# Moving a small mask transfer from the shared load queue to the ScalarE queue, with longer PE filler behind it

## Chip, cores and metric

One core of one Trainium2 chip. The metric is the device time of one execution in microseconds, median of several. Kernel before: 91.02 us (90.93 to 91.16). Runs agree within a few tenths of a per cent, so 2% is far outside the noise. In the traces PE is TensorE, DVE VectorE, ACT ScalarE, POOL GpSimd and SP SyncE; SPq and ACTq are the queues on which SP and ACT issue transfers. A filler is a matmul on zeros whose result nobody reads.

## The reference

```python
def setup_inputs():
    batch, m, k, n = 16, 512, 512, 512
    ...
        "mask": (np.triu(np.ones((m, n))) == 0).astype(np.float32),   # x, weight: float32

def reference(x, weight, scale, mask):
    y = scale * np.matmul(x, weight)
    y = np.where(mask == 1, y, -1e9)
    y_exp = np.exp(y - np.max(y, axis=-1, keepdims=True))
    return (y_exp / np.sum(y_exp, axis=-1, keepdims=True)).astype(np.float32)
```

16 MiB of x go in and 16 MiB of output go out, in 16 "units" of 1 MiB each (half the rows of two neighbouring matrices of the batch), beside 1 MiB of weights and the mask. Only the four 128 x 128 diagonal blocks of the mask are loaded: 512 runs of 512 bytes.

## The kernel before

```python
def load(u):
    xf = x_pool.tile([P, T, K], FP32, name="xf")                 # X_BUFS = 8 of these
    seq(nc.sync.dma_start(xf.rearrange("p t k -> p (t k)"), x_r[u // 2, u % 2]))
...
def store(u):
    ot = ots[u % OUT_BUFS]
    seq(nc.sync.dma_start(out_r[u // 2, u % 2], ot.rearrange("p t n -> p (t n)")))

load(0)
seq(nc.sync.dma_start(w_f32, weight.rearrange("(p kt) n -> p kt n", kt=KT)))
load(1)
seq(nc.sync.dma_start(diag_f32, diag_r))                         # the mask
for u in range(2, X_BUFS):
    load(u)
...
spin(12)                                                         # filler matmuls on zeros: keep the PE clock up
make_identity(nc, ident_bf)
...                                                              # "spread": four copies of the identity on ACT
cast(0); transpose(0); spin(16); evict(0)
...                                                              # weights to bf16
cast(1); transpose(1); spin(8); evict(1)
seq(nc.vector.tensor_scalar(out=diag_bf, in0=diag_f32, ...))     # needs the mask
for t in range(T):                                               # "band": additive mask, used by every unit
    seq(nc.tensor.matmul(pm, lhsT=spread[:, t], rhs=diag_bf..., start=True, stop=True))
    ...
for u in range(U + 1):                                           # the main loop
    ...                                                          # transpose u+1, cast u+2, evict u+1
    multiply(u)                                                  # matmuls, band added by one more matmul, exp
    normalise(u - 1); store(u - 1)
    if u - 1 + X_BUFS < U:
        load(u - 1 + X_BUFS)
```

All loads and stores go through one queue, SP's, in this order ("the line" below). A load can be issued only when its buffer is free, so beyond the first eight each load is issued right behind a store.

The softmax here doesn't subtract the row's maximum and nothing guards it: scores larger than these inputs give would overflow.

## Time and profile before

| | before |
|---|---|
| time, us | 91.02 |
| span in the profile, us | 89.1 |
| PE busy | 83% |
| DMA in the 40 slices | 9 tenths nearly throughout |
| main loop starts, us | 16.19 |
| first store issued, us | 21.50 |
| last store issued / landed, us | 80.1 / 88.05 |

Read it as two engines running side by side: PE has work without a gap from 16.2 to 77.5 us, and the line of transfers has work from 2.2 to 87.7 us. The lines that show this are in the prediction.

### The profile page before, as it was taken

To read this page: it belongs to the slowest core of one execution; us is meant where nothing else is said; L and a number is where in the kernel's file an instruction comes from. 1 tells how busy PE (TensorE), PEld (TensorE's weight loads), DVE (VectorE), ACT (ScalarE), POOL (GpSimd) and SP (SyncE) were. 2 spreads that over 40 slices of the span, in tenths; PEclk is the share of its full clock that TensorE was granted. 3 is DMA by queue.
4 is the path that set the end of the run, shared out by engine and by line. 5 is a ranking of instruction groups with operands and counts; after the bars stand their busy time and mean duration, and the time that the engine had idled before them with its cause. 6 is when DMAs were issued, how large, how long until landed. Compare 5 with 4: busy or idle time off the path is not lost.

```text
span 89.1 us, 1666 instructions
## 1 busy us (share of the span) xinstructions
PE 74.3 (83%) x616; PEld 50.0 (56%) x616; DVE 60.3 (68%) x123; ACT 55.0 (62%) x154; POOL 7.3 (8%) x20
## 2 busy tenths in 40 slices
PE   4967979899999999999999999999999999700000
PEld 1315454685795598579659847964984784300000
DVE  5876263989499779949977977967494999080000
ACT  5402604977697686969768786977778796710000
POOL 7620000002001000200100020002000102000000
PEclk9999999999999999999999999999999999995555
DMA  1899779999999999999999999999999999999970
GB/s 22 313 408 431 293 289 438 419 431 419 427 419 431 419 431 419 416 419 431 423 427 412 434 427 423 423 431 423 419 416 445 416 427 419 434 419 427 434 316 33
DMA packets 5287, 34.97 MB, mean 393 GB/s; under 512 B 544, under 2 KB 1056, under 8 KB 1056
## 3 DMA queue, kind: packets, MB, share of 16 engines
q1 hardware_dynamic: 5280, 34.87, 94.2%
q8 instruction: 5, 0.08, 0.3%
q14 instruction: 2, 0.02, 0.0%
HBM read 18.09 MB, written 16.78 MB: 392 GB/s over the span
## 4 chain that ended last, share of the span: by engine, by line
PE 72%; DMA 10%; DVE 4%; SPq 1%; ACT 1%; DVEq 0%; issue 0%; ACTq 0%
PE py L117 47%; PE pt L93 15%; DMA xf<-in_x_dram 10%; PE py L126 8%; PE py L175 2%; DVE ot L153 1%; DVE xb L84 1%; SPq L79 1%; ACT ot L136 1%; SPq L163 1%; DVE band L226 0%; DVEq L272 0%; ACT band L226 0%; PE py L219 0%; DVE rinv L151 0%
## 5 line engine op out<-in xcount | busy, mean ns | idle before, releaser
L117 PE MATMUL py<-w_bf,xt 128*128 128x256 bf16 (+1 forms) x256 | 49.4, 326 | 0.3 <-ACT band L226 0.3
L136 ACT ACTIVATE ot<-py 128x256 f32<-128x256 f32 (+1 forms) x64 | 31.2, 493 | 7.3 <-PE py L126 7.1
L117 PEld LDWEIGHTS <-xt 128*128 128x128 bf16 x256 | 24.4, 98 | 12.6 <-issue 0.5
L104 ACT COPY xt<-pt 128x1024 bf16<-128x1024 bf16 x16 | 16.2, 1012 | 13.6 <-PE pt L93 9.4
L84 DVE CAST xb<-xf 128x2048 bf16<-128x2048 f32 x16 | 19.5, 1220 | 7.2 <-DMA xf<-in_x_dram 7.2
L153 DVE TENSOR_SCALAR ot<-ot,rinv 128x256 f32<-128x256 f32 (+1 forms) x64 | 23.5, 431 | 0.8
L93 PE MATMUL pt<-ident_bf,xb 128*128 128x128 bf16 x256 | 17.0, 219 | 1.7 <-DVE xb L84 1.7
L93 PEld LDWEIGHTS <-xb 128*128 128x128 bf16 x256 | 15.9, 114 | 3.6 <-DVE xb L84 2.7
L126 PE MATMUL py<-band,ident_bf 128*128 128x256 bf16 x64 | 17.4, 273 | 0.0
L103 DVE COPY xt<-pt 128x1024 bf16<-128x1024 bf16 x16 | 11.0, 686 | 6.4 <-PE pt L93 6.4
L136 ACT ACTIVATION_READ_ACCUMULATOR ot<-py 128x1 f32 x64 | 12.8, 200 | 0.0
L175 PE MATMUL py<-zeros 128*128 128x512 bf16 x36 | 10.3, 447 | 1.2 <-DVE zeros L170 1.2
L155 POOL MEMSET ot<- 2x256 f32 x8 | 3.6, 449 | 65.8 <-DVE ot L153 65.8
L126 PEld LDWEIGHTS <-ident_bf 128*128 128x128 bf16 x64 | 6.3, 98 | 4.1
L175 PEld LDWEIGHTS <-zeros 128*128 128x128 bf16 x36 | 3.9, 112 | 6.3 <-issue 2.7
L151 DVE RECIPROCAL rinv<-rsum 128x4 f32<-128x4 f32 x16 | 2.7, 168 | 2.6 <-ACT ot L136 2.6
L183 DVE MEMSET ot<- 128x1024 f32 x4 | 3.6, 912 | 0.6 <-issue 0.6
L226 DVE CAST band<-py 64x256 bf16<-64x256 f32 x4 | 1.4, 408 | 1.4 <-PE py L219 1.4
L226 ACT CAST band<-py 64x256 bf16<-64x256 f32 x4 | 1.4, 367 | 1.4 <-DVE band L226 1.4
L190 ACT ACT_TABLE_LOAD x1 | 1.3, 1283 | 0.7 <-PEq L258 0.7
L184 POOL MEMSET ot<- 2x256 f32 x4 | 1.2, 301 | 1.5 <-DVE ot L183 1.4
L190 ACT COPY spread<-ident_bf 128x128 bf16<-128x128 bf16 x4 | 1.0, 330 | 0.2 <-POOL ident_bf masks.py:199 0.2
(14 smaller groups left out, 6.7 us busy)
## 6 DMA issues: line engine op xcount, KB each, us to landing
xf<-in_x_dram SPq DMA_DIRECT2D x16, 1024.0 KB, 14.9
out_dram<-ot SPq DMA_DIRECT2D x16, 1024.0 KB, 12.1
w_f<-in_weight_dram SPq DMA_DIRECT2D x1, 1024.0 KB, 7.0
diag_f<-in_mask_dram SPq DMA_DIRECT2D x1, 256.0 KB, 10.5
```

The source lines that it names most:

```text
L84: seq(nc.vector.tensor_copy(xb, st_x.pop(u)))
L93: nc.tensor.transpose(st_pt[u][kt // 2][:, kt % 2, t], xb[:, t].rearrange("p (k kt) -> p kt k", kt=KT)[:, kt], ident_bf,)
L103: seq(nc.vector.tensor_copy(xt[:, 0:2], pt[0]))
L104: seq(nc.scalar.copy(xt[:, 2:4], pt[1]))
L117: nc.tensor.matmul(py[:, :NC], lhsT=xt[:, kt, t], rhs=w_bf[:, kt, :NC], start=(kt == 0), stop=(kt == KT - 1),)
L126: nc.tensor.matmul(py[:, h * HB : NC], lhsT=ident_bf, rhs=band[:, h, t], start=False, stop=True, skip_group_check=True,)
L136: nc.scalar.activation(out=ot[:, t, :NC], in_=py[:, :NC], func=AF.Exp, bias=0.0, scale=float(scale), accum_out=rsum[:, t : t + 1],)
L153: seq(nc.vector.tensor_scalar_mul(ot[:, t, :NC], ot[:, t, :NC], rinv[:, t : t + 1]))
L155: seq(nc.gpsimd.memset(ot[0:2, 0, :HB], 1.0 / N))
L175: seq(nc.tensor.matmul(idle, lhsT=zeros[:, :P], rhs=zeros, start=True, stop=True))
L183: nc.vector.memset(ots[i][:, :, HB:], 0.0)
L226: seq(copy(band[half, :, t, g * P : (g + 1) * P], src[half, :, g]))
```

## The change

The intent: take the slow little mask transfer out of the line of loads, give it ScalarE's (ACT's) queue, let it flow "beside" the big loads, and bridge PE's longer wait for it with filler.

```diff
     load(0)
     seq(nc.sync.dma_start(w_f32, weight.rearrange("(p kt) n -> p kt n", kt=KT)))
-    load(1)
-    seq(nc.sync.dma_start(diag_f32, diag_r))
-    for u in range(2, X_BUFS):
+    for u in range(1, X_BUFS):
         load(u)
 ...                      # after the four spread copies
+    seq(nc.scalar.dma_start(diag_f32, diag_r))
 ...                      # after transpose(1)
-    spin(8)
+    spin(20)
```

## The prediction

> **What bounds the kernel now.** I read the slices first, then the DMA stretches, then the timeline of the start, then the waits of the DMA-issuing engine, and only then the chain of waits, because here the chain misleads. From the page:
>
> ```profile
> PE   4967979899999999999999999999999999700000
> DVE  5876263989499779949977977967494999080000
> DMA  1899779999999999999999999999999999999970
> GB/s 22 313 408 431 293 289 438 419 431 419 427 419 431 419 431 419 416 419 431 423 427 412 434 427 423 423 431 423 419 416 445 416 427 419 434 419 427 434 316 33
> PE py L117 47%; PE pt L93 15%; DMA xf<-in_x_dram 10%; PE py L126 8%; PE py L175 2%; DVE ot L153 1%; DVE xb L84 1%; SPq L79 1%; ACT ot L136 1%; SPq L163 1%; DVE band L226 0%; DVEq L272 0%; ACT band L226 0%; PE py L219 0%; DVE rinv L151 0%
> ```
>
> PE is full from the seventh slice to the thirty-fourth and the chain gives it 72%. But the last compute instruction is over at 80.1 us and the span is 89.1: the last tenth belongs to DMA alone, and the DMA row is at 9 almost throughout, with one dip, in slices five and six. The stretches show that dip, the waits of the issuing queue show the tail:
>
> ```profile
> core 0: us, PE busy (x) PEld busy (x) DVE busy (x) ACT busy (x) POOL busy (x), PEclk, DMA share, GB/s
> 4.20:10.20 6.00, 4.73 (x32) 2.40 (x31) 3.59 (x5) 1.83 (x2) 0.60 (x2) 1.00 1.00 419
> 10.20:12.40 2.20, 1.73 (x11) 0.65 (x9) 1.23 (x1) 0.13 (x1) 0.00 (x0) 1.00 0.58 160
> 12.40:85.00 72.60, 64.79 (x572) 45.82 (x570) 52.63 (x114) 50.81 (x147) 3.59 (x8) 0.97 1.01 425
> ```
>
> ```profile
> SPq L272 <- DMA out_dram<-ot: 7.3, 1, 7.3
> ```
>
> So all transfers form one line, served at 425 GB/s, and the kernel ends 7.3 us after the last store was issued because that store stands behind others. In the trace's landing records the last two stores land at 85.61 and 88.05, 2.44 us apart, which is 1 MiB at full rate: still a backlog. The first bound is the DMA line; PE is a second bound close behind it. In the middle they touch: the casts of the last four x tiles, up to the one at 68.51 us, each start on a landing, yet PE never runs dry.
>
> The start, from the timeline:
>
> ```profile
> 2.18 0.96 ACT L190 COPY spread<-ident_bf 128x128 bf16<-128x128 bf16 x4 [0.16 <-POOL ident_bf masks.py:199]
> 2.69 0.70 SPq L165 DMA_DIRECT2D diag_f<-in_mask_dram  x1
> 10.97 1.23 DVE L84 CAST xb<-xf 128x2048 bf16<-128x2048 f32 x1 [1.75 <-DMA xf<-in_x_dram]
> 12.26 1.08 PE L93 MATMUL pt<-ident_bf,xb 128*128 128x128 bf16 x16 [0.47 <-DVE xb L84]
> 13.18 1.89 PE L175 MATMUL py<-zeros 128*128 128x512 bf16 x8
> 13.54 0.42 DVE L207 TENSOR_SCALAR diag_bf<-diag_f 128x512 bf16<-128x512 f32 x1
> 14.91 1.03 PE L219 MATMUL py<-diag_bf,spread 128*128 128x512 bf16 x4
> 16.19 0.60 PE L117 MATMUL py<-w_bf,xt 128*128 128x256 bf16 x4 [0.26 <-ACT band L226]
> ```
>
> The mask is issued at 2.69 and, by its row of the issues (10.5 us to landing), lands at 13.2, in time: the conversion at 13.54 does not wait for it. Converted at 13.96, it is ready before the eight filler matmuls end (the chain starts L219 at 15.07). The main loop starts at 16.19.
>
> **What the Trainium skill says.** (1) "DMA: Bandwidth & Descriptors", section "Issuing engines are not separate DMA queues": transfers from the scalar and sync engines run on the same 16 DMA engines and interleave; a second issuer only saves sequencer time. No run yet shows a second queue here; the issue costs 0.6 to 0.7 us. (2) Same page, "Queues, rings and completion order": each DMA engine takes turns between the queues that have work, a packet at a time. The trace of before has one data queue and cannot confirm it; my landing time for the mask rests on it. (3) Same page, "Why small descriptors are slow (HBM only)": small descriptors cost a fixed overhead each. The trace shows far more than that: the mask is 512 packets of 512 B, 32 per engine, mostly 27 ns each, so 0.86 us an engine, but x tile 1 and x tile 2, with the mask between, land 4.67 us apart where neighbours are 2.48 apart. The mask takes 2.19 us of the line; some 1.3 us of that the engines stand idle. (4) "TensorE: Matmul & The Clock Gate", "Wait — 56ns, not 53.3ns?": 215.7 ns from start to start for N = 512 with a warm clock. The trace agrees: eight fillers take 15.07 - 13.34 = 1.73 us on the chain, 0.216 each.
>
> **The change part by part.**
>
> The mask leaves the SP line. It is now the fifth instruction of ACT, right after the four spread copies, with no semaphore wait before it (the instruction order shows this). So it is issued at about 2.18 + 0.96 = 3.15, only 0.45 us later than before, but on a queue of its own: it no longer stands behind w and x tile 1, it alternates with them. ACT is idle until its eviction at 8.37, so 0.7 us of issue costs it nothing.
>
> Removed from the line: the idle part. In 10.2 to 12.4 us 160 GB/s moved instead of 425, which is 2.2 x (1 - 160/425) = 1.37 us lost. With an 8192 B packet (309 ns) between any two mask packets the wait for one should lie under the other. I credit 1.3 us to the DMA line; the 0.6 to 0.9 us of true mask data stay. If nothing else bound, the last landing would go from 88.05 to about 86.75, and the time to 89.7.
>
> x tile 1 comes later. First packets appeared 1.43 us after the first issue (2.17 against 0.74), so mask packets begin near 4.6. Up to the end of tile 1's data, some 10.2, there are 5.6/0.336 = 17 turns of one 309 and one 27 ns packet, and 17 x 27 ns = 0.46 us of delay. I take 0.45 us: landing 11.4 instead of 10.95, and with it the cast and transposes of tile 1.
>
> The mask comes later too: 32 turns x 0.336 = 10.75 us, so about 15.4, plus 0.5 us for the completion: 15.9 instead of 13.2. Converted by 16.3.
>
> Added: 12 fillers, in program order ahead of L219, 12 x 0.216 = 2.6 us on PE. The transposes end at 13.34 + 0.45 = 13.8, the twenty fillers at 13.8 + 20 x 0.216 = 18.1. The mask (16.3) is ready by then, so the fillers and not the mask decide when L219 starts: 18.1 instead of 15.07, 3.05 us later. Everything from there on is the same PE work: 77.46 - 16.19 = 61.3 us without a gap. So the main loop starts at 19.2, the last multiplication ends at 80.5, and the last store is issued at about 83.15 instead of 80.1.
>
> The sum. The DMA line alone would gain 1.3 us. Compute is 3.05 us later. How much of that is on the path? The last store had slack, because it stood in the backlog. Issued on an empty line a 1 MiB transfer needs 1.43 us to its first packet and 2.47 us (8 x 309 ns) of data, plus 0.5 us or more: 4.4 us at least; the first x tile, the only one here that found an empty line, took 5.2. So the last store lands between 83.15 + 4.4 = 87.55 and 83.15 + 5.2 = 88.35, against 88.05 now. The line, at 85.61 - 1.3 = 84.3 for the store before, is free by its first packet at 84.6. So the end passes from the DMA line to PE plus one uncovered store, at 87.95 in the middle: 0.1 us less than now. Time 91.02 - 0.1 = 90.9; I lean to 91.1 because the start of an empty line was slow (first packets of 400 to 770 ns).
>
> Does the line run dry earlier? The first store would be issued at 21.50 + 3.05 = 24.55, first packet near 26.0; the queued x loads end about 28.0 - 0.5 - 1.3 = 26.2. Just covered, by 0.2 us. The second store: 26.31 + 3.05 + 1.43 = 30.8 against 26.2 + 5.0 = 31.2. Covered; later ones have more room.
>
> **The rivals.** (a) The DMA saving reaches the end: 89.7. It needs the later start to be harmless; against it stand 2.6 us of fillers in program order before the main loop and only about 3 us of slack in the last store. The landing of the last store bounds this. (b) The mask is served much more slowly than one packet a turn, say two x packets for each of its own: then it lands near 26, PE waits some 8 us behind the fillers, the line runs dry at 26 and the time is 96 or more. For it: nothing in this trace shows the turns. Against it: twenty fillers end at 18.1, a length chosen as if the mask came a little before. (c) The mask is served in a burst: then it lands by 8, tile 1 is delayed by up to 0.86 us rather than 0.45, and the time is near 91.5; the long filler is pure loss. (d) The idle part of the mask does not overlap: the line gains nothing, ends at 88.05 as before, and the uncovered store is as above: 91.0 to 91.4.
>
> **Range and chances.** (a) to (d) without (b) lie between 89.7 and 91.5. The filler's 2.6 us is nearly certain, so I put the low end at 90.3 and keep room above for a drying line and a later mask: 92.5. Faster by over 2% (below 89.2) is under what even the DMA line allows: 0.03. Slower by over 2% (above 92.84) needs the mask to be converted at 19.9 or later: 0.12. Within 2%: 0.85.
>
> **What would show it.** Right: the mask's issue takes about 12.7 us to landing; the dip in slices five and six is gone; L219 starts near 18.1 right behind the fillers; L117 near 19.2; the issuing queue's last wait for a store falls from 7.3 to about 4.2. Wrong: a PE gap between the fillers and L219 with the mask's conversion as its releaser; a new dip near 26 us; a last wait still near 7, which would mean that the line is the bound and the mask's cost stayed in it.

## The result and the profile after

93.58 us (93.52 to 93.72, 4 runs) against 91.02: a ratio of 1.028, 95% interval 1.026 to 1.030. (Ratios here are the mean time of one kernel's fast runs over that of the other's of the same rounds, so not quite the ratio of the medians.) It is slower, and outside the range I gave. Executions over 1.5% slower than the fastest of the same kernel are left out of the means.

From the page of the changed kernel, the rows that answer to those of before:

```profile
PE   4988929989999999999999999999999999940000
DMA  1899999999999999999999999999999999999940
GB/s 32 300 418 291 408 372 425 424 421 428 414 414 343 375 411 393 332 421 389 418 435 418 432 414 439 418 432 421 425 418 439 411 439 414 432 418 403 403 186 11
q10 hardware_dynamic: 528, 0.26, 1.0%
```

The dip that stood in slices five and six is gone from the DMA row, as intended, and the mask is on its own queue, q10. But the GB/s row shows that the DMA engines are "busy" and slow: 291 and 372 near 8 and 13 us, and new dips of 343, 375, 393, 332 between 27 and 39 us, where before stood 416 to 431.

The start, selected lines from the timeline of the changed kernel:

```profile
2.19 0.45 ACTq L195 DMA_DIRECT2D diag_f<-in_mask_dram  x1
12.24 1.23 DVE L84 CAST xb<-xf 128x2048 bf16<-128x2048 f32 x1 [2.37 <-DMA xf<-in_x_dram]
14.45 4.48 PE L173 MATMUL py<-zeros 128*128 128x512 bf16 x20
18.35 0.43 DVE L208 TENSOR_SCALAR diag_bf<-diag_f 128x512 bf16<-128x512 f32 x1 [3.46 <-DMA diag_f<-in_mask_dram]
18.83 1.02 PE L220 MATMUL py<-diag_bf,spread 128*128 128x512 bf16 x4
20.11 0.60 PE L117 MATMUL py<-w_bf,xt 128*128 128x256 bf16 x4 [0.26 <-ACT band L227]
25.10 0.61 SPq L159 DMA_DIRECT2D out_dram<-ot  x1
```

The mask lands at 18.3 instead of 13.1; DVE waits 3.5 us for it. The fillers and the mask end together, and the main loop starts at 20.11 instead of 16.19, 3.9 us later. The first store goes out at 25.10 instead of 21.50. PE is then full as before.

The same stretches for both kernels, the kernel before first. Columns: length, busy time of PE, PEld, DVE, ACT, POOL, clock, DMA share, GB/s.

```profile
10.20:12.40 2.20, 1.73 (x11) 0.65 (x9) 1.23 (x1) 0.13 (x1) 0.00 (x0) 1.00 0.58 160
12.40:22.00 9.60, 9.34 (x78) 6.18 (x77) 7.33 (x15) 6.41 (x18) 0.45 (x1) 1.00 1.02 429
27.00:32.00 5.00, 5.00 (x43) 3.07 (x41) 3.84 (x9) 3.67 (x9) 0.45 (x1) 1.00 1.02 429
32.00:38.00 6.00, 6.00 (x54) 4.34 (x52) 5.93 (x14) 4.88 (x14) 0.45 (x1) 1.00 1.01 419
```

```profile
4.20:10.20 6.00, 5.17 (x32) 2.37 (x31) 3.69 (x5) 1.75 (x2) 0.60 (x2) 1.00 0.97 367
10.20:12.40 2.20, 1.67 (x8) 0.59 (x6) 0.16 (x1) 0.21 (x1) 0.00 (x0) 1.00 0.99 396
12.40:22.00 9.60, 8.21 (x58) 4.96 (x59) 4.95 (x9) 3.27 (x10) 0.00 (x0) 1.00 1.00 415
27.00:32.00 5.00, 5.00 (x59) 4.31 (x58) 4.24 (x9) 3.98 (x12) 0.00 (x0) 1.00 0.97 357
32.00:38.00 6.00, 6.00 (x53) 4.34 (x52) 4.81 (x13) 4.90 (x16) 0.45 (x1) 1.00 1.02 386
```

Multiply length by GB/s to get KB. From 4.2 to 22 us the kernel before moved 6.0 x 419 + 2.2 x 160 + 9.6 x 429 = 6984 KB, the changed one 6.0 x 367 + 2.2 x 396 + 9.6 x 415 = 7057 KB. The whole gain of the mixing is 73 KB, 0.17 us at 425 GB/s, where I had credited 1.3 us. From 27 to 38 us it is 5 x 429 + 6 x 419 = 4659 against 5 x 357 + 6 x 386 = 4101 KB: 558 KB or 1.3 us lost, with PE full in both.

A mean hides what ends the kernel. A transfer runs on 16 DMA engines, and each reports its own landing. First, median and last engine, in us, from the trace's landing records:

```
                     before                  after
x tile 7        26.94 27.54 29.23      27.31 27.42 28.96
store 0         29.38 30.05 31.71      30.02 30.28 31.46
x tile 8        31.81 32.47 34.11      32.60 32.95 35.60
store 1         34.36 35.05 36.61      35.22 35.53 38.04
x tile 9        36.75 37.50 39.01      38.09 38.29 41.70
store 14        83.23 84.35 85.61      84.82 85.60 88.36
store 15        85.68 86.79 88.05      88.07 88.22 90.80
```

The last engine ends at 90.80 instead of 88.05: 2.75 us. By steps: up to x tile 7 it is 0.27 ahead; from x tile 7 to x tile 9 it takes 12.74 instead of 9.78 us, 2.96 lost; from there to store 14 46.66 against 46.60; the last store 2.44 in both. So the loss happens between 28 and 42 us, at the first stores and the loads between them, and is never made up. The packets show what it is: one of 8 KB normally takes 309 ns, and of the 75 that start between 28 and 30 us 19 take 600 to 625.

The last store is issued at 84.03, and nine of the 16 engines land it between 88.07 and 88.26, some 4.1 us later, without a backlog. The seven others are still behind, up to 2.7 us, and the last of them sets the end of the kernel. The issuing queue's wait for that store, 7.3 us before, is now:

```profile
SPq L273 <- DMA out_dram<-ot: 6.2, 1, 6.2
```

### The profile page after: what moved, and what is told of

It reads as the page before. It is cut to its first block, busy times and chain, and to the rows that moved or that the text cites. A ratio compares the mean times of both kernels' runs of the same rounds, so it can differ in the third digit from the quotient of the medians.

```text
span 91.8 us, 1690 instructions
## 1 busy us (share of the span) xinstructions
PE 77.4 (84%) x628; PEld 51.2 (56%) x628; DVE 60.5 (66%) x123; ACT 55.1 (60%) x154; POOL 7.3 (8%) x20
## 4 chain that ended last, share of the span: by engine, by line
PE 73%; DMA 11%; DVE 3%; SPq 1%; ACT 1%; issue 0%; DVEq 0%; ACTq 0%
PE py L117 45%; PE pt L93 15%; DMA xf<-in_x_dram 11%; PE py L126 8%; PE py L173 5%; DVE ot L153 1%; DVE xb L84 1%; SPq L79 1%; ACT ot L136 1%; SPq L163 1%; DVE band L227 0%; DVEq L273 0%; ACT band L227 0%; PE py L220 0%; DVE rinv L151 0%
## 5 line engine op out<-in xcount | busy, mean ns | idle before, releaser
L93 PEld LDWEIGHTS <-xb 128*128 128x128 bf16 x256 | 15.9, 113 | 4.8 <-DVE xb L84 3.9
L173 PE MATMUL py<-zeros 128*128 128x512 bf16 x48 | 13.4, 442 | 1.2 <-DVE zeros L168 1.2
L173 PEld LDWEIGHTS <-zeros 128*128 128x128 bf16 x48 | 5.1, 110 | 7.7 <-issue 2.8
```

Of the source, the lines that this page charges most:

```text
L93: nc.tensor.transpose(st_pt[u][kt // 2][:, kt % 2, t], xb[:, t].rearrange("p (k kt) -> p kt k", kt=KT)[:, kt], ident_bf,)
L173: seq(nc.tensor.matmul(idle, lhsT=zeros[:, :P], rhs=zeros, start=True, stop=True))
```

## The experiments

My theory after seeing this, S: the loss comes from the late start of the main loop, which issues the first stores when the line of queued loads is nearly used up. Rivals: Q, the alternating second queue itself disturbs the DMA engines; F, the fillers cost their 2.6 us straight.

### Filler alone, and the same late start without the second queue

`d1_sp_fill20`: kernel before with `spin(8)` made `spin(20)`.

> The kernel before, mask on the SP queue, but 20 fillers instead of 8: main loop from 16.19 to about 18.8. Theory S (what costs is the later start of the main loop: stores come when the line of queued loads has run out, and DMA engines fall behind): first store issued near 24.1 with the queued loads lasting to about 27.5, so still covered; 91.0 to 91.6. Theory Q (the second queue itself costs, by slowing the loads it alternates with): 91.0. Theory F (the 12 fillers cost their 2.6 us straight): 93.6.

91.05 us, ratio 1.001 (0.999 to 1.003). Twelve fillers are free here: F falls. Main loop at 18.71, first store at 23.69.

`d2_sp_fill26`: kernel before with `spin(26)`.

> The kernel before with 26 fillers, mask on the SP queue: main loop near 20.1, the same start as the changed kernel has (20.11). S: as slow as the changed kernel, 93.2 to 93.9, with packets of about 600 ns near 28 us and a spread of over 3 us between the DMA engines at the end. Q: 91.0 to 91.4, only the last store uncovered. F: 94.9.

93.69 us, ratio 1.030 (1.027 to 1.033). The mask is on the old queue, and still the time is that of the changed kernel. Its main loop starts at 20.09, and its stretches show the same loss:

```profile
20.09 0.60 PE L117 MATMUL py<-w_bf,xt 128*128 128x256 bf16 x4 [0.26 <-ACT band L226]
27.00:32.00 5.00, 4.95 (x59) 4.30 (x59) 4.26 (x9) 4.00 (x12) 0.00 (x0) 1.00 1.04 406
32.00:38.00 6.00, 6.00 (x54) 4.35 (x52) 4.81 (x13) 4.90 (x16) 0.45 (x1) 1.00 1.00 362
```

Q is not needed. Six more fillers than in `d1`, 1.4 us of start, cost 2.6 us.

`d3_act_fill8`: changed kernel with

```diff
-    spin(20)
+    spin(8)
```

> The changed kernel (mask on the ACT queue) with 8 fillers instead of 20. S and Q: the mask still lands near 18.3 and PE waits for it, so the main loop starts near 20.1 as with 20 fillers: 93.4 to 93.9, a little more if the clock drops in the PE gap of about 2.6 us. F: 91.0.

93.95 us, ratio 1.033 (1.029 to 1.038). PE waits for the mask instead of turning over:

```profile
18.45 1.02 PE L220 MATMUL py<-diag_bf,spread 128*128 128x512 bf16 x4 [2.49 <-DVE diag_bf L208]
19.73 0.76 PE L117 MATMUL py<-w_bf,xt 128*128 128x256 bf16 x4 [0.26 <-ACT band L227]
```

and a little later the granted clock is about half (0.51, 0.50 and 0.50 in the microseconds from 20 to 23), so the first store goes out at 26.39, later still. With this the two parts of the change stand in a square: 8 fillers, SP queue 90.9; 20 fillers, SP queue 91.05; 8 fillers, ACT queue 93.95; 20 fillers, ACT queue 93.58. The whole loss comes with the move of the mask, and given the move the fillers make no difference that is clear of the noise (intervals 1.029 to 1.038 without them, 1.026 to 1.030 with them).

`f4_sp_fill23`: kernel before with `spin(23)`, between the two.

> The kernel before with 23 fillers: main loop near 19.45, midway between the harmless start (18.8, 91.05) and the costly one (20.1, 93.69). S with a gradual loss: 92.0 to 92.7. S with an edge: either about 91.1 or about 93.2. Start times alone without a short line (1.3 us for 1.3 us): 91.7.

92.40 us, the median of three fast runs (92.22 to 92.90; a fourth, at 93.83, counts as slow), ratio 1.017 (1.014 to 1.021), which at 2% leaves the verdict unclear. It lies between the two, so the loss looks gradual rather than like an edge. In its trace store 0 flows nearly at full speed, and the slow packets come later, mostly between 36 and 37 us: x tile 9, behind store 1, lands on its last engine 3.8 us after that store instead of 2.4.

### Take away what makes the start late, or what makes it hurt

`e7_act_unused`: the mask goes through ACT's queue as in the change, but nothing waits for it.

```diff
-    seq(nc.scalar.dma_start(diag_f32, diag_r))
+    seq(nc.scalar.dma_start(diag_un, diag_r))        # a tile that nobody reads
+    nc.gpsimd.memset(diag_f32, 1.0)                  # with the early POOL work: the blocks on chip,
+    nc.gpsimd.affine_select(out=diag_f32, ...)       # right for this mask only
-    spin(20)
+    spin(8)
```

> The changed kernel's mask transfer on the ACT queue, but into a tile that nothing reads; the diagonal blocks are made on chip by POOL (for this mask only) and there are 8 fillers. x tile 1 still lands near 12.2, the main loop starts near 17.4, because nothing waits for the mask. S: no short line, 90.8 to 91.3. Q: the mask's turns between the loads cost as much as in the changed kernel, 93.0 to 93.8.

90.74 us, ratio 0.997 (0.995 to 0.999). The second queue, the turns and x tile 1 landing at 12.05 are all there, and the kernel is a trace faster than before. Q falls.

`e5_act_x10`: changed kernel with

```diff
-X_BUFS = 8
+X_BUFS = 10
```

> The changed kernel with 10 x buffers instead of 8, so 10 loads are queued before the first store and the line lasts some 5 us longer; mask, fillers and main-loop start (about 20.1) as in the changed kernel. Theory S (the line runs short at the first stores): the slow stretches near 28 and 37 us go, and the time falls to 91.0 to 91.6, set by the last store issued near 84.0. Theory Q (the alternating queue has put the DMA engines out of step for good): stays 93.3 to 93.8.

90.96 us, ratio 0.9995 (0.998 to 1.001). Mask, fillers, main loop (20.07) and first store (25.06) are those of the changed kernel; two more loads stand in the queue ahead of that store, and the loss is gone:

```profile
27.00:32.00 5.00, 4.95 (x59) 4.30 (x59) 4.27 (x9) 4.01 (x12) 0.00 (x0) 1.00 1.01 423
32.00:38.00 6.00, 6.00 (x54) 4.34 (x52) 4.82 (x12) 4.89 (x16) 0.45 (x1) 1.00 1.01 421
SPq L273 <- DMA out_dram<-ot: 3.6, 1, 3.6
```

The last line is the last wait for a store: 3.6 us, against 6.2 in the changed kernel. Here (and nearly so in `f3` below) the kernel ends as I had predicted for the change: the last store stands uncovered (all engines land it between 88.05 and 88.21), and DMA and PE end together.

`f3_act_x9`: the same with `X_BUFS = 9`.

> The changed kernel with 9 x buffers: one load more ahead of the first store, 2.5 us of line. S: one tile is already more than the 1.3 us between a harmless start (18.8) and a costly one (20.1): 90.9 to 91.4. If the line needs both tiles: 92 or more.

91.06 us, ratio 1.001 (1.000 to 1.003). One tile more is enough.

`e6_sp_x10`: the control, kernel before with `X_BUFS = 10`.

> The kernel before with 10 x buffers. The line is never short there, so S: unchanged, 90.8 to 91.1. If deeper queueing helps by itself: below 90.5, and e5 would have to be read against this run.

91.06 us, ratio 1.001 (0.999 to 1.003). More buffers by themselves bring nothing.

### The mask elsewhere, or nowhere

`e8_act_top`: changed kernel with the mask issued before everything else.

```diff
+    seq(nc.scalar.dma_start(diag_f32, diag_r))
     load(0)
 ...
-    seq(nc.scalar.dma_start(diag_f32, diag_r))
-    spin(20)
+    spin(8)
```

> Mask on the ACT queue as ACT's first instruction, ahead of the table load, with 8 fillers. The mask should land at 12 to 15, with x tile 0, w and x tile 1 each somewhat later; main loop near 16.5 to 17.5. S: 90.8 to 91.3, no better than before because the mask's share of the line stays. A rival hope, that mixing hides the mask's idle DMA time after all: 89.7 to 90.2.

93.53 us, the median of the three fast runs (93.37 to 93.84), 1.028 (1.026 to 1.031): above my range by 2.2 us. One of its four executions took 444 us, with every PE instruction several times as long; that was the profiled one, and I have no cause for it.

`f2_act_top_again`: the same kernel.

> The kernel with the mask as ACT's first instruction once more, because its profile fell into a slow state. One look: 93.3 to 93.8 again. S: x tile 0 and all behind it land late (x tile 0 near 8.8 instead of 5.9), so that the main loop starts at 19.5 or later and the slow stretches near 28 and 37 us are there. If the main loop starts before 18.8, S does not explain this run.

93.89 us, one run. Stretches of its first microseconds:

```profile
2.00:3.00 1.00, 1.00 (x4) 0.42 (x3) 0.84 (x2) 0.99 (x4) 0.94 (x2) 1.00 0.45 102
3.00:4.00 1.00, 1.00 (x4) 0.34 (x3) 0.84 (x2) 0.45 (x3) 0.71 (x3) 1.00 0.61 113
```

The mask lands at 6.4, but the line moves 102 and 113 GB/s in its first two microseconds instead of 213 and 328, and x tile 0 lands near 8.9 instead of 5.9. Everything behind it is 3 us late: the main loop starts at 20.53, and the dips near 28 and 37 us are back. The miss comes from these first microseconds, in which the packets of the mask and of x tile 0 pass side by side; why that costs so much was not tested. The loss after it is the one that S describes.

`d4_no_mask`: kernel before without the transfer, the blocks made on chip as in `e7` (an experiment, since it ignores the mask that is passed in).

> No mask transfer: the four diagonal blocks are made on chip by POOL, for this mask only (an experiment, not a solution). 8 fillers, main loop near 16.2. If the line of transfers is the bound and the mask took 2.19 us of it: 88.7 to 89.0. If it is not the bound: 91.0.

89.58 us, ratio 0.985 (0.983 to 0.987). The line is the bound, but only 1.4 of the mask's 2.19 us came back: here too stands a slow stretch, in x tile 7, from 23.3 to 25.3 us.

`f1_no_mask_x10`: that kernel with `X_BUFS = 10`.

> No mask transfer and 10 x buffers. Without the mask and with 8 buffers only 1.4 of the 2.19 us came back, and slow packets stood near 24 us, before the first store. If that loss too is the short line (theory S), 10 buffers bring the rest: 88.7 to 89.0, no slow stretch. If it is something else: 89.5 as with 8.

90.42 us, ratio 0.993 (0.992 to 0.995). A plain miss of S. Ten loads are queued and the first store goes out at 21.48, some 9 us before they are done, and yet:

```profile
27.00:32.00 5.00, 4.95 (x43) 3.08 (x42) 3.85 (x9) 3.67 (x10) 0.45 (x1) 1.00 0.98 365
```

The slow packets now sit in x tile 9, again the last load ahead of the first store. So they belong to the change from loads to stores, and a short queue is not the only thing that brings them.

### A second theory for the slow packets, and its fall

P: the slow packets come when all 16 DMA engines pass from loads to stores nearly in step. In the first traces the engines landed x tile 6 within 0.3 to 0.6 us of each other where slow packets followed (one late engine left out), and 0.7 to 1.1 apart where they did not. (I overlooked `f2`, which has slow packets with its engines 2.2 us apart.) Three small extra transfers that use only some of the engines should set them apart:

```diff
         load(u)
+        if u == 3:
+            for o, rows in ((7, 4), (5, 2), (3, 1)):     # output tiles overwritten later
+                seq(nc.sync.dma_start(ots[o][: 2 * rows]..., x_r[0, 0, :rows]))
```

`g1_act_skew`: changed kernel with this.

> The changed kernel with three extra small transfers after x tile 3 (8, 4 and 2 rows of 8 KB into output tiles that are overwritten later), which should set the DMA engines 0, 0.3, 0.6 and 0.9 us apart before the first store. Theory P (the slow stretch comes when the 16 engines pass from loads to stores nearly in step; in the runs with it they were 0.3 to 0.6 us apart, in those without 0.7 to 1.1): no slow stretch, 91.0 to 92.0. Theory S (a short line alone): 93.5 to 94.3.

94.36 us, ratio 1.037 (1.033 to 1.041). The engines are now up to 2.6 us apart at x tile 6, and the 606 ns packets are there all the same.

`g2_no_mask_skew`: the kernel without the mask with this.

> No mask, 8 buffers, with the same three small transfers. P: no slow stretch near 24 us, 88.8 to 89.4. S or another cause: 89.6 to 90.4, the 1.3 us of loss stays and the extra transfers add to it.

91.07 us, ratio 1.000 (0.997 to 1.003). Also slow packets, near 25 us. It is slower than either theory said; the extra transfers cost more than their bytes, and I did not follow that up.

`g4_after_again` and `g5_before_again`: second traces of the two kernels.

> The changed kernel unaltered, for a second trace. If the slow stretches belong to the program: again near 28 and 37 us, last store's DMA engines about 2.7 us apart. P: the engines land x tile 6 within 0.6 us of each other (one late engine left out); S says nothing of that.

> The kernel before unaltered, for a second trace. No slow stretch after 13 us. P: the engines land x tile 6 over 0.65 us apart again (one late engine left out).

93.76 and 90.97 us. The changed kernel shows its dips again, with the engines 0.6 us apart at x tile 6; the kernel before shows none, with the engines only 0.5 us apart. P falls: the distance differs from run to run, the loss does not.

### What the runs with a mask have in common

Take the time from the issue of the first store to the landing (median engine) of the last load queued ahead of it:

```
kernel              first store   last queued load   difference   time, us
d3_act_fill8           26.39           27.32             0.9        93.95
f2_act_top_again       25.51           27.07             1.6        93.89
after                  25.10           27.42             2.3        93.58
g1_act_skew            25.44           27.89             2.4        94.36
g4_after_again         24.86           27.33             2.5        93.76
d2_sp_fill26           25.07           27.67             2.6        93.69
f4_sp_fill23           24.49           27.57             3.1        92.40
d1_sp_fill20           23.69           27.48             3.8        91.05
f3_act_x9              24.90           29.84             4.9        91.06
e7_act_unused          22.27           27.44             5.2        90.74
before                 21.50           27.54             6.0        91.02
g5_before_again        21.35           27.51             6.2        90.97
e5_act_x10             25.06           32.30             7.2        90.96
e6_sp_x10              21.43           32.54            11.1        91.06
```

At 3.8 us and more nothing is lost, at 2.6 and less 2.6 us or more. That is well above the 1.7 us at which the line would run dry: 1.3 from a store's issue to its first packet (in d3, where the line did run dry, 26.39 to 27.66) and 0.4 from the last packet of a transfer to its landing (87.69 to 88.05 at the end of the kernel before). The three kernels without a mask transfer do not fit this table.

## Why the prediction was wrong

**Late mask and late tile 1: right in kind, too small.** I expected one mask packet to each load packet, and so it is on average: the 512 mask packets pass between 6.3 and 17.5 us, beside 488 of 8 KB, 0.35 us a turn against the 0.336 that I reckoned. But they begin at 6.3 and not at 4.6, although ACT issued the mask at 2.19, a microsecond sooner than I thought. The mask lands at 18.3 instead of 15.9, x tile 1 at 12.2 instead of 11.4, the main loop starts at 20.1 instead of 19.2.

**"I credit 1.3 us to the DMA line": wrong.** It gained 0.17 us; rival (d), that the idle part of the mask does not overlap, had this term right. Mixed with the loads, the mask no longer leaves the engines idle; it makes the packets beside it slower instead (8 KB packets average 366 and 351 ns in 6 to 8 and 8 to 10 us, against 309). x tile 7 lands at 27.42 instead of 27.54. The mask's 2 us stay in the line wherever it is queued: d4 shows what leaving it out is worth, and even that not in full.

**Fillers: right in cost, not on the path.** They take PE time as reckoned, but d1 shows that on the old queue the later start they bring costs nothing.

**"Just covered, by 0.2 us": the step that failed.** I asked only whether the queue of loads would be empty before the first store's first packet, counted 26.0 against 26.2, and took "not empty" for "no loss". With the times of the trace it was not empty either, 26.4 (25.10 + 1.3) against about 27.0 (27.42 - 0.4), and still 1.3 us went on average and 3.0 us on the last engine. The margin from the first store's issue to the last queued landing that keeps the line whole was between 3.1 and 3.8 us; my reckoning asked for 1.9 (1.43 to the first packet, 0.5 for the completion). Before the change the margin was 6.0, which is why I could not see the edge in that profile; the change spent 3.7 of it. e5 and f3 show the step by giving the margin back. Two of the signs of being wrong that I had named came: a new dip, near 28 us, and a last wait of 6.2 us instead of about 4.2.

**The uncovered last store: right for half of the engines.** I put its landing at 87.95. Nine engines land it at 88.07 to 88.26. That this is so near is partly luck: the store was issued at 84.03 and not at 83.15, and took 4.0 to 4.2 us to land and not the 4.4 to 5.2 that I allowed. I read the line as one thing that serves 425 GB/s, but it is 16 engines that each keep their own delay, and the last of them, at 90.80, sets the time. The landing records of the kernel before already showed such a lag, which I left out: x tile 7 landed at 29.23 on its last engine, where I reckoned with 28.0. The lag is the term that turns a predicted gain of 0.1 us into a loss of 2.6.

**Open.** What slows the packets at the change from loads to stores is not settled. A line that is short fits all kernels with a mask transfer and fails for the three without; engines in step fail too. The runs settle that the late start of the main loop, with eight buffers, brings it in this change, that it costs 2.6 us, and that one more buffer removes it. Whether it is the first store itself that comes too late, or the load issued right behind it, they do not separate.

No version that reads the mask beat the kernel before: the best, `e5`, stands at 0.9995 (0.998 to 1.001).

## What to carry to other kernels

In this kernel, where one queue carries everything and is the bound, a later start of the compute was free only while the first results were issued well ahead of the end of the queued loads; that took over 3 us, more than twice the latency from issue to first packet. Measure that margin before moving anything that the start of the loop waits for; if it shrinks, try one more input buffer, which was enough here. A large margin is no guarantee, though: the kernels without the mask had slow packets with 5 us (`d4`) and 9.6 us (`f1`) of it. And moving an inefficient little transfer to another queue did not make it cheap: it delayed its neighbours, and it arrived 5.2 us later, since it got only about every second turn.

## What the Trainium skill lacked or had wrong

- "DMA: Bandwidth & Descriptors", "Specifications": it names 512 B as the least size for line rate. The mask's 512 B packets took 2.19 us for 256 KB on the line, some 120 GB/s where 8 KB packets move 425 GB/s, and mixing them with 8 KB packets won back only 0.17 us. Taken alone, the row misleads here; the section on small descriptors that the prediction cites does warn of a fixed cost for each.
- Same page, "Queues, rings and completion order": engines take turns between queues, with typically 9 to 17 descriptors to a packet. Here the trace has 511 packets of 512 B beside 488 of 8 KB between 6.3 and 17.5 us, so about one run of the mask to one of x, 0.35 us a turn; 32 of them per engine took 11.2 us. The section does not say what makes up a turn for transfers like these.
- Same page, "Latency and other measured facts": about 0.6 us to the first byte, without saying from when. Counted from the start of the issuing instruction the first transfer of the kernel took 1.43 us to its first packet and a store on an empty line 1.27 (d3); counted from the end of that instruction they took 0.77 and 0.67, close to the page. The mask on the second queue, with loads already queued on the first, took 4.1 us (2.19 to 6.29), which the page does not cover.
- No page that I used has the slow stretch at the change from queued loads to the first stores: 606 ns packets instead of 309, up to 3 us lost on one engine (changed kernel, 28 to 42 us).
- No page that I used says that a delay on one DMA engine stays with it until a kernel that keeps its queue full ends, nor that it comes with an instruction fetch. Such a delay, of some 1.2 us, goes in time with such a fetch, of 16 KB (five in each trace): in the kernel before the first fetch starts at 20.78 us, and x tile 5 lands at 23.08 on the fifteenth engine and at 24.29 on the last; in the changed kernel it starts at 24.50, and the first tile with such a gap is x tile 6 (25.15 and 26.66). In the kernel before the delay was still there 10 us later.
